# Pads that move the matmul operands of a two-layer encoder trunk to 0 or 32 modulo 256 bytes

## The chip, the core and the metric

The kernel runs on one core of a Trainium2 chip. The metric is the time of one execution in microseconds (us). TensorE multiplies: it first loads a stationary tile of 128x128 (a weight load, PEld in the profile) and then streams a moving tile past it (a matmul, PE). VectorE (DVE), ScalarE (ACT), GpSimd (POOL) and the queue of SyncE (SP), which issues the loads, work beside it. All operands lie in the on-chip memory, 128 partitions wide; an address here is a byte offset within a partition, the same in all of them.

## The reference

Two layers over 256 tokens of width 2048, all in float32. Layer 0 mixes tokens with a convolution module, layer 1 with latent attention; behind each comes an MLP with squared ReLU, and an RMS norm stands before each sub-layer and at the end.

```python
for layer in range(2):
    h = rms_norm(x, norm_mixer_g[layer])
    if layer == 0:   # h @ w_pw1, GLU, causal depthwise conv (width 31), layer norm, swish, @ w_pw2
        x = x + conv_module(h, ...)
    else:            # low-rank q and kv, rotary key, 16 heads, block-causal mask, @ w_o
        x = x + mla(h, cos, sin, ...)
    h = rms_norm(x, norm_mlp_g[layer])
    x = x + jnp.square(jax.nn.relu(h @ mlp_w1[layer])) @ mlp_w2[layer]   # 2048 -> 8192 -> 2048
return rms_norm(x, final_norm_g)
```

## The kernel before

**Products in three parts.** TensorE's one-pass format (float32r) keeps fewer bits than float32. So each operand is split in a high part and the rest (`hi` and `lo` of the weights, `xh`/`xl`, `gh`/`gl`, `sh`/`sl_`, `kvh`/`kvl`, `qh`/`ql`, `oh`/`ol` of the activations), and a product is high by high, low by high and high by low, summed in one accumulator. `mm3` (L177 to L179) does this with activations stationary and weights moving:

```python
nc.tensor.matmul(ps, sh, mh, start=start, stop=False)   # L177
nc.tensor.matmul(ps, sl, mh, start=False, stop=False)   # L178
nc.tensor.matmul(ps, sh, ml, start=False, stop=stop)    # L179
```

**Weights.** Each weight comes in units of up to 1 MB. SP loads a unit into one of three `raw` buffers. ScalarE copies it to `hi` (L151), VectorE (POOL in the first stage) subtracts to get `lo` (L152), in halves, with six buffers for each. The loads run ahead as buffers come free; the order of instructions on the engines is the order of the program.

**Stages.**
- First convolution product (L479 to L481, 1536 matmuls of 256 columns): weights stationary, `xh`/`xl` (tile `xt`) moving. Beside it run the depthwise taps in full float32 (L512 on TensorE, tiles `dg` and `ub`; the rest on VectorE).
- Second convolution product (384 matmuls of 512 columns): `sh`/`sl_` stationary, weights moving. Half of it runs in the convolution's own loop, half in `product_A`.
- MLP, twice. The first product is 1024 pairs a layer: a 512-wide matmul of `hi` against `xh` and `xl` side by side (L394), then a 256-wide one of `lo` against `xh` (L395). The squared ReLU gives `gh`/`gl`. The second product is `product_A`, 1536 `mm3` matmuls a layer, 512 wide, `gh`/`gl` stationary, weights moving.
- Attention: the input product on `xt` as stationary (192 matmuls of 288 columns and 96 of 512); the up-projections with `kvh`/`kvl` and `qh`/`ql` (moving in L964 to L966 and L987 to L989, stationary in `mm3`; 672 matmuls of 256 columns); scores and values in full float32 on the tiles of pool `gp`; and the output product with `oh`/`ol` stationary (384 matmuls of 512 columns), part of it between the heads, part in `product_A`.

In `product_A` the innermost loop is

```python
for j in range(4):
    k = 4 * u + j
    for t in range(T):
        mm3(ps[t], hi(k, t), lo(k, t), *wjs[u](j), k == 0, k == nk - 1)
```

**Addresses.** Pools lie one behind the other on the left side of the memory; the pools opened with `side="right"` (`edge`, then `xt` or `gp`) grow down from the top. Two small tiles on the left (`pad_const`, `pad_small`) and one on the right (`pad_right`) hold nothing that is read; their sizes set where the next tiles begin. Nearly all steps inside a tile are multiples of 256 bytes, so that a tile's start modulo 256 is that of each slice. An exception is the weights of the attention's input product, whose two column halves are 1152 bytes apart.

| tiles | start modulo 256 before |
|---|---|
| weights `hi`, `lo` (behind `pad_const`) | 0 |
| `sh`, `sl_`, `gh`, `gl` (behind `pad_small`) | 128 |
| `xt`, and `kT`, `qT`, `qpT`, `vv`, `pT` in `gp` (below `pad_right`) | 128 |
| `kvh`, `kvl`, `qh`, `ql`, `kpT` | 0 |
| `oh`, `ol` | 0 |

Of the kernel before, what the change touches and what calls it, by code (L numbers as in the profile page):

```python
# [10 lines left out]
F32 = mybir.dt.float32  # L11
# [7 lines left out]
P = 128  # L19
# [15 lines left out]
CHUNK = 64  # L35
HALVES = 2
PAD_CONST = 24
PAD_SMALL = 16
PAD_RIGHT = 24
WB = 6  # L40
LOOK = WB // 2 - 1
PE_TAPS = (3, 3, 3, 3)
# [28 lines left out]
def trunk_kernel(  # L71
# [26 lines left out]
    nc = tc.nc  # L98
# [13 lines left out]
            psum[kind] = psum_cx[0].enter_context(tc.tile_pool(name=kind + name, bufs=n, space=PSUM, reuse_waits="tile"))  # L112

    ctx.callback(lambda: psum_cx[0].close())


    const.tile([P, PAD_CONST], F32, name="pad_const")
    small.tile([P, PAD_SMALL], F32, tag="pad_small", name="pad_small", bufs=1)
    edge = ctx.enter_context(tc.tile_pool(name="edge", bufs=1, side="right"))
    pad_right = edge.tile([P, PAD_RIGHT], F32, name="pad_right")  # L120
    nc.gpsimd.memset(pad_right, 0.0)
# [699 lines left out]
    with ExitStack() as cx:  # L821
        at = cx.enter_context(tc.tile_pool(name="at", bufs=1, reuse_waits="tile"))
# [63 lines left out]
        def u_load(n):  # L886
            if n < len(units):
                srcs, shape = units[n]
                raw = raws[n] = wpool.tile(shape, F32, tag="raw", name=nm("raw"), bufs=3)
                for i, src in enumerate(srcs):  # L890
                    dst = raw if len(srcs) == 1 else raw[:, i : i + 1, :]
                    if len(src.shape) == 4:
                        dst = dst.rearrange("p j (h n) -> p j h n", h=src.shape[2])
                    nc.sync.dma_start(dst, src)
# [18 lines left out]
        def prefetch(n=9):  # L913
            while pending and n > 0:
# [3 lines left out]
                if h == 1:  # L918
                    u_load(u + 3)

        kvh = at.tile([P, KR // P, S], F32R, name="kvh")
        kvl = at.tile([P, KR // P, S], F32R, name="kvl")
        qh = at.tile([P, QR // P, S], F32R, name="qh")
        ql = at.tile([P, QR // P, S], F32R, name="ql")
        kpT = at.tile([P, S], F32, name="kpT")
        oh = at.tile([P, H, S], F32R, name="oh")
        ol = at.tile([P, H, S], F32R, name="ol")

# [325 lines left out]
```

## Time and profile before

| | |
|---|---|
| time, median of 3 runs | 2067.19 us (2066.62 to 2067.25) |
| profiled execution | 2066.48 us, of which the span from the first to the last instruction is 2064.7 |
| TensorE busy | 99% of the span, 11132 matmuls and as many weight loads |
| granted TensorE clock | 0.998 |

In the profile, PE is the matmul, PEld its weight load. A row of a group gives line, engine, operation, output and inputs, shapes and count; then busy time in us, the mean ns of one, and the idle time ahead with what ended it. Matmuls overlap, so the mean of one is longer than the distance from one to the next. The timeline gives start and duration in us.

### The profile page before, as it was taken

The numbers are of one execution on the slowest core, as the hardware profiler recorded it, in microseconds if no ns is written. First come the engines' busy times: TensorE is split into PE (matmuls) and PEld (weight loads), VectorE is DVE, ScalarE is ACT, GpSimd is POOL, SyncE is SP. The second block draws the span as 40 slices with busy tenths as digits, with TensorE's granted clock in tenths as the row PEclk, the third lists the DMA queues.
The fourth block names the chain that finished last, engine by engine and source line by source line (L and its number), as shares of the span: only waits on it lengthen the run. The fifth ranks groups of instructions, "written<-read, shape, count | busy, mean of one in ns | idle before, by whom it ended". The sixth has DMA issues, their size and how long they took to land.

```text
span 2064.7 us, 27877 instructions
## 1 busy us (share of the span) xinstructions
PE 2041.7 (99%) x11132; PEld 1753.7 (85%) x11132; DVE 1217.6 (59%) x1820; ACT 951.7 (46%) x1325; POOL 173.3 (8%) x99
## 2 busy tenths in 40 slices
PE   7999999999999999999999999999999999999998
PEld 7999888888888888888889887888888888888886
DVE  5999866665544465555446655665654445565454
ACT  5444565544433354444445544554443334454442
POOL 5887300000000000000000000000000000000000
PEclk9999999999999999999999999999999999999999
DMA  7555355565555665555555344566655555555552
GB/s 231 164 164 164 123 185 183 185 188 193 188 184 190 191 190 184 185 192 187 179 166 165 107 138 147 190 197 190 194 185 185 191 193 186 184 185 192 193 184 102
DMA packets 243267, 367.59 MB, mean 178 GB/s; under 512 B 15416, under 2 KB 89792, under 8 KB 242880
## 3 DMA queue, kind: packets, MB, share of 16 engines
q1 hardware_dynamic: 242400, 364.68, 55.0%
q8 instruction: 87, 1.43, 0.3%
q10 hardware_dynamic: 736, 1.12, 0.2%
q14 instruction: 44, 0.36, 0.0%
HBM read 363.68 MB, written 2.10 MB: 177 GB/s over the span
## 4 chain that ended last, share of the span: by engine, by line
PE 98%; DVE 1%; DMA 0%; ACT 0%; issue 0%; SPq 0%; DVEq 0%; ACTq 0%
PE acc L394 23%; PE acc L177 16%; PE acc L179 16%; PE acc L178 16%; PE acc L395 12%; PE acc L481 3%; PE acc L480 3%; PE acc L479 3%; PE sum L512 1%; PE acc L1042 1%; PE tr L234 1%; PE acc L1041 1%; PE acc L964 0%; PE acc L987 0%; PE acc L966 0%; PE acc L965 0%
## 5 line engine op out<-in xcount | busy, mean ns | idle before, releaser
L152 DVE TENSOR_TENSOR lo<-raw,hi 128x1024 fp32r<-128x1024 f32 (+1 forms) x628 | 755.4, 1206 | 710.3 <-ACT hi L151 695.8
L151 ACT ACTIVATE hi<-raw 128x1024 fp32r<-128x1024 f32 (+1 forms) x696 | 722.0, 1045 | 820.3 <-PE acc L178 475.0
L394 PE MATMUL acc<-xt,hi 128*128 128x512 f32 x2048 | 719.5, 394 | 0.0
L395 PE MATMUL acc<-xt,lo 128*128 128x256 f32 x2048 | 579.4, 283 | 0.0
L394 PEld LDWEIGHTS acc<-xt,hi 128*128 128x128 f32 x2048 | 384.6, 188 | 88.7
L177 PE MATMUL acc<-hi,gh 128*128 128x512 f32 x1024 | 404.3, 395 | 0.0
L179 PE MATMUL acc<-lo,gh 128*128 128x512 f32 x1024 | 404.1, 395 | 0.0
L178 PE MATMUL acc<-hi,gl 128*128 128x512 f32 x1024 | 404.0, 395 | 0.0
L395 PEld LDWEIGHTS acc<-xt,lo 128*128 128x128 f32 x2048 | 385.0, 188 | 0.1
L179 PEld LDWEIGHTS acc<-lo,gh 128*128 128x128 f32 x1024 | 192.9, 188 | 45.0
L177 PEld LDWEIGHTS acc<-hi,gh 128*128 128x128 f32 x1024 | 192.9, 188 | 44.9
L178 PEld LDWEIGHTS acc<-hi,gl 128*128 128x128 f32 x1024 | 192.9, 188 | 44.9
L546 DVE SCALAR_TENSOR_TENSOR sum<-ub,w_dw,sum 128x256 f32<-128x256 f32 x402 | 167.7, 485 | 4.9 <-ACT sum L515 2.9
L152 POOL TENSOR_TENSOR lo<-raw,hi 128x1024 fp32r<-128x1024 f32 x68 | 161.6, 2398 | 60.1 <-ACT hi L151 60.1
L479 PE MATMUL acc<-xt,hi 128*128 128x256 f32 x512 | 148.3, 290 | 0.0
L481 PE MATMUL acc<-xt,lo 128*128 128x256 f32 x512 | 144.3, 282 | 0.6 <-POOL lo L152 0.6
L480 PE MATMUL acc<-xt,hi 128*128 128x256 f32 x512 | 144.2, 282 | 0.0
L481 PEld LDWEIGHTS acc<-xt,lo 128*128 128x128 f32 x512 | 96.4, 188 | 0.8 <-POOL lo L152 0.8
L480 PEld LDWEIGHTS acc<-xt,hi 128*128 128x128 f32 x512 | 96.5, 188 | 0.6 <-DVE xt L190 0.2
L479 PEld LDWEIGHTS acc<-xt,hi 128*128 128x128 f32 x512 | 96.5, 188 | 0.4
L402 ACT ACTIVATE v<-acc 128x256 f32<-128x256 f32 x128 | 46.8, 383 | 26.1 <-PE acc L395 26.1
L177 PE MATMUL acc<-hi,sh 128*128 128x512 f32 x128 | 51.3, 400 | 0.0
(198 smaller groups left out, 1673.0 us busy)
## 6 DMA issues: line engine op xcount, KB each, us to landing
raw<-in_mlp_w SPq DMA_DIRECT2D x256, 1024.0 KB, 5.1
raw<-in_conv_w_pw SPq DMA_DIRECT2D x64, 512.0 KB, 4.9
raw<-in_conv_w_pw SPq DMA_DIRECT2D x16, 1024.0 KB, 5.0
raw<-in_mla_w_o SPq DMA_DIRECT2D x16, 1024.0 KB, 5.5
raw<-in_mla_w_kv_up SPq DMA_DIRECT2D x8, 1024.0 KB, 5.4
raw<-in_mla_w_in SPq DMA_DIRECT2D x8, 576.0 KB, 3.7
raw<-in_mla_w_in SPq DMA_DIRECT2D x4, 1024.0 KB, 4.9
raw<-in_mla_w_q_up SPq DMA_DIRECT2D x16, 256.0 KB, 3.2
```

The lines of the kernel that those rows point to most:

```text
L151: nc.scalar.activation(hi, raw[:, js, :], AF.Copy)
L152: eng.tensor_tensor(lo, raw[:, js, :], hi.bitcast(F32), op=ALU.subtract)
L177: nc.tensor.matmul(ps, sh, mh, start=start, stop=False)
L178: nc.tensor.matmul(ps, sl, mh, start=False, stop=False)
L179: nc.tensor.matmul(ps, sh, ml, start=False, stop=stop)
L394: nc.tensor.matmul(ps[b], wh[:, bs], xhl(k), start=k == 0, stop=False)
L395: nc.tensor.matmul(ps[b][:, :S], wl[:, bs], xh(k), start=False, stop=k == KC - 1)
L402: nc.scalar.activation(v[:, b, :], o[:, S:], AF.Copy)
L479: nc.tensor.matmul(o, wh[:, bs], xh(k), start=k == 0, stop=False)
L480: nc.tensor.matmul(o, wh[:, bs], xl(k), start=False, stop=False)
L481: nc.tensor.matmul(o, wl[:, bs], xh(k), start=False, stop=k == KC - 1)
L546: nc.vector.scalar_tensor_tensor(out=out, in0=ubs[c][:, w : w + S], scalar=tap(c, w), in1=pcs[c], op0=ALU.mult, op1=ALU.add)
```

## The change

Three constants get another size, and two pad tiles are put into the attention's pool, each cleared once by POOL. No other instruction changes.

```diff
-PAD_SMALL = 16
-PAD_RIGHT = 24
+PAD_SMALL = 48
+PAD_RIGHT = 48
+PAD_KV = 40
+PAD_O = 56
...
+        pad_kv = at.tile([P, PAD_KV], F32, name="pad_kv")
+        nc.gpsimd.memset(pad_kv, 0.0)
         kvh = at.tile([P, KR // P, S], F32R, name="kvh")
         kvl = at.tile([P, KR // P, S], F32R, name="kvl")
         qh = at.tile([P, QR // P, S], F32R, name="qh")
         ql = at.tile([P, QR // P, S], F32R, name="ql")
         kpT = at.tile([P, S], F32, name="kpT")
+        pad_o = at.tile([P, PAD_O], F32, name="pad_o")
+        nc.gpsimd.memset(pad_o, 0.0)
         oh = at.tile([P, H, S], F32R, name="oh")
         ol = at.tile([P, H, S], F32R, name="ol")
```

By the sizes (four bytes an element), `sh`, `sl_`, `gh` and `gl` move from 128 to 0, `xt` and the tiles of `gp` from 128 to 32, `kvh`, `kvl`, `qh`, `ql` and `kpT` from 0 to 32; `hi`, `lo`, `oh` and `ol` stay at 0. The stationary address minus the moving one, modulo 256:

| product | before | after |
|---|---|---|
| first convolution product, first MLP product (weights stationary, `xt` moving) | 128 | 224 |
| second convolution product, second MLP product (`mm3`) | 128 | 0 |
| attention's input product (`xt` stationary) | 128, for the second column half 0 | 32, second half 160 |
| up-projections, weights stationary | 0 | 224 |
| up-projections, weights moving | 0 | 32 |
| attention's output product | 0 | 0 |

## The prediction

> **What bounds the kernel now.** I read the page's busy shares and its chain first, then the groups of instructions with the shapes kept apart, then the timeline of TensorE alone, in which the starts of neighbouring matmuls give what the durations hide.
>
> ```profile
> span 2064.7 us, 27877 instructions
> PE 2041.7 (99%) x11132; PEld 1753.7 (85%) x11132; DVE 1217.6 (59%) x1820; ACT 951.7 (46%) x1325; POOL 173.3 (8%) x99
> POOL 5887300000000000000000000000000000000000
> GB/s 231 164 164 164 123 185 183 185 188 193 188 184 190 191 190 184 185 192 187 179 166 165 107 138 147 190 197 190 194 185 185 191 193 186 184 185 192 193 184 102
> PE 98%; DVE 1%; DMA 0%; ACT 0%; issue 0%; SPq 0%; DVEq 0%; ACTq 0%
> core 0: 2064.7 us, clock 0.998
> ```
>
> The chain that ended last is TensorE for 98%, at a granted clock of 0.998. No other engine has to be mended: the time is the sum of the distances from one matmul's start to the next (its pitch), and a change that moves only addresses can act on nothing else.
>
> ```profile
> L152 DVE TENSOR_TENSOR lo<-raw,hi 128x1024 fp32r<-128x1024 f32 x604 | 737.9, 1225 | 690.8 <-ACT hi L151 676.4 <-PE tr L234 10.1 <-DMA raw<-in_mla_w_kv_up 2.4
> L394 PE MATMUL acc<-xt,hi 128*128 128x512 f32 x2048 | 719.5, 394 | 0.0
> L151 ACT ACTIVATE hi<-raw 128x1024 fp32r<-128x1024 f32 x672 | 706.2, 1059 | 800.5 <-PE acc L178 455.3 <-PE acc L394 310.8 <-ACT gh L406 29.3
> L178 PE MATMUL acc<-hi,gl 128*128 128x512 f32 x1024 | 404.0, 395 | 0.0
> L178 PE MATMUL acc<-hi,ol 128*128 128x512 f32 x128 | 49.9, 390 | 0.0
> ```
>
> The last two rows are the same instruction on the same shape: one line, 512 columns, 128x128 stationary. One takes 395 ns, the other 390. In the first the stationary tile `gl` lies at 128 modulo 256 bytes, in the second `ol` lies at 0; the moving weights lie at 0 in both. I call D the stationary address minus the moving one, modulo 256: 128 in the first row, 0 in the second. Durations overlap, so I take pitches from the timeline (start in us, duration, operation). The second MLP product, 62 rows, 61 steps:
>
> ```profile
> 559.77 0.39 PE L178 MATMUL acc<-hi,gl 128*128 128x512 f32 x1
> ...
> 573.95 0.40 PE L179 MATMUL acc<-lo,gh 128*128 128x512 f32 x1
> ```
>
> 14.18 / 61 = 232.5 ns at D = 128. The attention's output product, 34 rows, 33 steps, D = 0:
>
> ```profile
> 1304.32 0.39 PE L178 MATMUL acc<-hi,ol 128*128 128x512 f32 x1
> ...
> 1311.80 0.39 PE L178 MATMUL acc<-hi,ol 128*128 128x512 f32 x1
> ```
>
> 7.48 / 33 = 226.7 ns. So the trace already holds both layouts in the same loop (`product_A`), and D = 0 is 5.8 ns a matmul cheaper. The Trainium skill, page "TensorE: Matmul & The Clock Gate", section "Part 2: What happens when you issue a matmul", says that the stationary and the moving operand have independent read ports, so that loading the next stationary tile takes nothing from the running matmul. By that rule alone D could not matter and the time would stay at 2067; these two pitches disagree with it by 5.8 ns.
>
> **The change part by part.** Pads alone move; no instruction on TensorE, ScalarE, VectorE or in a queue is added or dropped but two memsets on POOL. By the sizes of the pads: PAD_SMALL adds 128 bytes ahead of everything behind the small pool, PAD_RIGHT takes 96 bytes off everything on the right side, `pad_kv` (160) and `pad_o` (224) shift the attention's tiles.
>
> *1. Second MLP product, 3072 matmuls (L177 to L179 on gh, gl).* Stationary 128 becomes 0, moving stays 0: D goes from 128 to 0, the pair of addresses of the oh rows. 3072 x 5.8 = 17.8 us off the path. The other end: D = 0 isn't always at 226.7. Behind a break the pitch stays higher for a while (9 rows, 8 steps):
>
> ```profile
> 1270.99 0.40 PE L179 MATMUL acc<-lo,oh 128*128 128x512 f32 x1
> ...
> 1272.84 0.39 PE L178 MATMUL acc<-hi,ol 128*128 128x512 f32 x1
> ```
>
> 1.85 / 8 = 231.3 ns, a gain of 1.2 ns, 3.7 us in all if the matmuls never settled. I take 17.8: the loop of the 1304 us rows is the very loop that term 1 runs, and there it had settled.
>
> *2. Second convolution product, 384 matmuls (sh, sl).* The same move, D 128 to 0: 384 x 5.8 = 2.2 us (0.5 at 1.2 ns).
>
> *3. First MLP product, 2048 pairs of a 512- and a 256-wide matmul (L394, L395).* Here the weights are stationary at 0 and xt moves: 128 becomes 32, D goes from 128 to 224. No row has D = 224 in this shape. Now, 30 rows of L394, 29 pairs:
>
> ```profile
> 399.72 0.39 PE L394 MATMUL acc<-xt,hi 128*128 128x512 f32 x1
> 399.94 0.28 PE L395 MATMUL acc<-xt,lo 128*128 128x256 f32 x1
> 400.06 0.40 PE L394 MATMUL acc<-xt,hi 128*128 128x512 f32 x1
> 400.30 0.28 PE L395 MATMUL acc<-xt,lo 128*128 128x256 f32 x1
> ...
> 409.90 0.40 PE L394 MATMUL acc<-xt,hi 128*128 128x512 f32 x1
> ```
>
> 10.18 / 29 = 351.0 ns a pair; the 512-wide ones swing between 0.22 and 0.24 us in one and the same layout, so a good part of the price is where in time the weight load meets the stream, not the bytes alone. 256-wide at D = 0 (key and value up-projection, 51 rows, 50 steps) and at D = 128 (first convolution product, 45 rows, 44 steps):
>
> ```profile
> 1112.10 0.28 PE L964 MATMUL acc<-kvh,hi 128*128 128x256 f32 x1
> ...
> 1118.10 0.28 PE L966 MATMUL acc<-kvh,lo 128*128 128x256 f32 x1
> ```
> ```profile
> 99.72 0.28 PE L480 MATMUL acc<-xt,hi 128*128 128x256 f32 x1
> ...
> 104.94 0.28 PE L479 MATMUL acc<-xt,hi 128*128 128x256 f32 x1
> ```
>
> 6.00 / 50 = 120.0 ns and 5.22 / 44 = 118.6 ns. D = 224 is 32 bytes from D = 0 and 96 from D = 128, so I price it as D = 0, its nearest row: 226.7 + 120.0 = 346.7 ns a pair, 4.3 ns off, 2048 x 4.3 = 8.9 us. Ends: a stream that isn't disturbed at all. The nearest row is the taps' product in full fp32, which reads its moving columns twice, each matmul with its own weight load:
>
> ```profile
> 34.33 1.29 PE sum L512 x6
> ```
>
> 1.29 / 6 = 215 ns for what amounts to 512 columns, about 108 for 256: a pair of 323, 57 us off. The other end: every 512-wide one at the slow beat of the rows above (400.06 to 400.30, 0.24 us) beside 0.12: 360 a pair, 18 us more.
>
> *4. First convolution product, 1536 matmuls 256 wide (L479 to L481).* Also D 128 to 224, by the same row 120.0 for 118.6: 1.4 x 1536 = 2.2 us more. Ends: 108 (16 us off) and the same 1.4 ns once again (4.3 us more).
>
> *5. Low-rank up-projections of the attention, 672 matmuls 256 wide (kvh, kvl, qh, ql).* D goes from 0 to 224 where they move and to 32 where they are stationary; the pitch is 120.0 now and I leave it: 0. Ends: 8 us off at 108, 0.9 us more at 1.4 ns each.
>
> *6. Attention's input product.* 192 matmuls 288 wide; their moving half-rows are 1152 bytes apart, so that D alternates between 128 and 0 already (47 rows, 46 steps):
>
> ```profile
> 1073.53 0.29 PE L179 MATMUL acc<-lo,xt 128*128 128x288 f32 x1
> ...
> 1079.66 0.30 PE L177 MATMUL acc<-hi,xt 128*128 128x288 f32 x1
> ```
>
> 133.3 ns each, whichever D: 0. The 96 that are 512 wide go from D = 128 to 32: 0, within 0.6 us. Scores, values, taps and transposes shift with both operands or run at half speed: 0. The output product's oh and ol stay at 0: 0.
>
> *7. The memsets of the two pads.* POOL is idle from the eighth slice on (the POOL row), nothing is queued behind them there, and no matmul reads the pads: 0. Without that cover some 2.6 us, by POOL's nearest simple operation:
>
> ```profile
> L686 POOL TENSOR_TENSOR xs<-xs,b 128x512 f32<-128x512 f32 x8 | 10.4, 1295 | 0.0
> ```
>
> *What is late next.* A unit of weights (1 MB) feeds 24 matmuls of 226.7 = 5.4 us. ScalarE needs 2 x 1.06 and VectorE 2 x 1.23 us for it, and both stand idle 691 to 800 us in these lines. 1 MB in 5.4 us is 193 GB/s; the first slice moved 231. So the supply keeps up.
>
> Sum: -17.8 - 2.2 - 8.9 + 2.2 = -26.7 us. The profiled run took 2066.5 us (its span is 2064.7), 0.7 under the median of 2067.2: 2039.8 for it, 2040.5 for the median.
>
> **The rivals.**
>
> *A. The 32-byte offset does more than D = 0.* For it: taps show that a weight load and a stream can pass at 215. Against: no row of a one-pass matmul is there. Halfway to the floor: 512 wide at 221, 256 wide at 114, a pair of 335: -32.8, convolution -7.1, up-projections -4.0, with -20.0 of terms 1 and 2: 2067.2 - 63.9 = 2003.
>
> *B. D = 224 acts as D = 128 does*, and only the stationary moves pay (terms 1 and 2): 2067.2 - 20.0 = 2047. For it: at 256 columns D = 0 and 128 differ by only 1.4 ns, so the offset may matter in few places.
>
> *C. The address isn't the cause.* The oh rows might be quick because of what else runs there. Against: same loop, same loads and splits beside it. Then 2067. The rule quoted above would say the same.
>
> *D. Slower.* A stream that starts at 32 modulo 256 begins inside what may be a larger unit of reading. 6016 matmuls would have such a moving operand (4096 + 1536 + 384). It decides from 20.0 / 6016 = 3.3 ns each; at 5.8 ns, what 128 bytes do above, it is +34.9 - 20.0: 2082. For it: every one-pass stream of the trace starts at 0 or 128, so it's untried. Against: the taps' streams start at 4-byte steps and hold 215.
>
> **How the numbers follow.** Forecast 0.46, A 0.22, B 0.18, C 0.06, D 0.08. A measurement of this kernel can tell about 0.2%, 4 us. Faster are the forecast, A and B: 0.86; C is the same: 0.06; D slower: 0.08. The forecast's own range is 2033 to 2046 (its terms 3 to 5 within 6 us). The range for 8 in 10 takes in B and the nearer half of A and leaves out C, D and the far end of A: 1998 to 2053.
>
> **What would show it.** Right: L177 to L179 on gh and gl at 390 instead of 395 ns and a pitch near 226.7; L394 with L395 at 347 a pair; the first convolution product near 120. Rival A would show L394 well under 390 ns and a pair near 335, B the old 351, D more than 355. Term 1 is wrong if the gh pitch stays near 231, as behind the break at 1271 us. The chain should stay TensorE at 98%; a new idle time before L177 or L394 released by VectorE or DMA would mean that the supply had become late after all.

## The result, and the profile after

The changed kernel runs in 2034.74 us (median of four, 2034.44 to 2036.34) against 2067.07 (four runs, 2066.62 to 2067.25): 32.3 us less, a ratio of 0.9845 with a 95% interval of 0.9828 to 0.9863. The profiled execution took 2034.44 us, its span is 2032.6, 32.1 below the span of before. The page of after, its busy shares and its chain:

```profile
span 2032.6 us, 27882 instructions
PE 2009.5 (99%) x11132; PEld 1747.1 (86%) x11132; DVE 1214.8 (60%) x1820; ACT 951.7 (47%) x1325; POOL 174.2 (9%) x101
PE 98%; DVE 1%; DMA 0%; ACT 0%; issue 0%; SPq 0%; DVEq 0%; ACTq 0%
```

As many matmuls and weight loads as before, TensorE still 98% of the chain, VectorE and ScalarE within 3 us of what they were. The 32 us are TensorE's own. The groups of instructions, shapes kept apart (the three lines of `mm3` are L180 to L182 now, the first MLP product's L397 and L398):

```profile
L397 PE MATMUL acc<-xt,hi 128*128 128x512 f32 x2048 | 710.5, 390 | 0.0
L398 PE MATMUL acc<-xt,lo 128*128 128x256 f32 x2048 | 577.7, 282 | 0.0
L180 PE MATMUL acc<-hi,gh 128*128 128x512 f32 x1024 | 398.6, 389 | 0.0
L181 PE MATMUL acc<-hi,gl 128*128 128x512 f32 x1024 | 398.4, 389 | 0.0
L182 PE MATMUL acc<-lo,gh 128*128 128x512 f32 x1024 | 398.4, 389 | 0.0
```

The `gl` row has come from 395 to 389 ns, to within 1 ns of what the `ol` row of the same line had all along. L398 tells of the limit of such rows: 283 became 282, while its pitch fell by 2.2. So here too the pitch is read from the timeline of TensorE (start in us, duration, operation). The second MLP product, 63 rows, 62 steps:

```profile
544.80 0.39 PE L181 MATMUL acc<-hi,gl 128*128 128x512 f32 x1
...
558.86 0.39 PE L180 MATMUL acc<-hi,gh 128*128 128x512 f32 x1
```

14.06 / 62 = 226.8 ns, where it was 232.5. The first MLP product, 30 rows of L397, 29 pairs:

```profile
399.89 0.39 PE L397 MATMUL acc<-xt,hi 128*128 128x512 f32 x1
400.12 0.28 PE L398 MATMUL acc<-xt,lo 128*128 128x256 f32 x1
400.24 0.39 PE L397 MATMUL acc<-xt,hi 128*128 128x512 f32 x1
...
409.95 0.39 PE L397 MATMUL acc<-xt,hi 128*128 128x512 f32 x1
```

10.06 / 29 = 346.9 ns a pair instead of 351.0. The first convolution product, 51 rows, 50 steps:

```profile
99.12 0.28 PE L482 MATMUL acc<-xt,hi 128*128 128x256 f32 x1
...
104.96 0.28 PE L484 MATMUL acc<-xt,lo 128*128 128x256 f32 x1
```

5.84 / 50 = 116.8 ns instead of 118.6. And the up-projection with `kvh` moving, 24 rows, 23 steps:

```profile
1098.53 0.28 PE L971 MATMUL acc<-kvh,hi 128*128 128x256 f32 x1
...
1101.21 0.28 PE L973 MATMUL acc<-kvh,lo 128*128 128x256 f32 x1
```

2.68 / 23 = 116.5 ns instead of 120.0. Summed over the whole timeline, from the start of each matmul of a product to the start of the next matmul (us; in brackets the mean in ns):

| product | before | after | difference | predicted |
|---|---|---|---|---|
| second MLP (3071 steps) | 714.1 (232.5) | 696.5 (226.8) | -17.6 | -17.8 |
| second convolution (384) | 90.3 (235.2) | 88.3 (229.9) | -2.0 | -2.2 |
| first MLP, 512 wide (2048) | 472.4 (230.7) | 467.9 (228.5) | -4.5 | |
| first MLP, 256 wide (2048) | 247.0 (120.6) | 242.5 (118.4) | -4.5 | -8.9 for both |
| first convolution (1536) | 189.1 (123.1) | 186.6 (121.5) | -2.5 | +2.2 |
| up-projections (672) | 82.8 (123.2) | 81.4 (121.2) | -1.3 | 0 |
| attention's input product, output product, all else | 250.5 | 251.0 | +0.5 | 0 |

These means are over the whole product, breaks included, so they lie above the settled pitches where blocks are short. Nothing has become late in exchange: the longest wait of TensorE in the view of waits is still the load at the start, and the next is 1.2 us.

```profile
PE tr L276 <- DMA stage<-in_conv_b_dw: 8.6, 1, 8.6
PE sum L515 <- DVE ub L500: 1.2, 1, 1.2
```

### The profile page after: what moved, and what is told of

Its sections match the earlier page's. It is cut to its first block, busy times and chain, and to the rows that moved or that the text cites. A ratio compares the mean times of both kernels' runs of the same rounds, so it can differ in the third digit from the quotient of the medians.

```text
span 2032.6 us, 27882 instructions
## 1 busy us (share of the span) xinstructions
PE 2009.5 (99%) x11132; PEld 1747.1 (86%) x11132; DVE 1214.8 (60%) x1820; ACT 951.7 (47%) x1325; POOL 174.2 (9%) x101
## 4 chain that ended last, share of the span: by engine, by line
PE 98%; DVE 1%; DMA 0%; ACT 0%; issue 0%; SPq 0%; DVEq 0%; ACTq 0%
PE acc L397 23%; PE acc L180 16%; PE acc L182 16%; PE acc L181 16%; PE acc L398 12%; PE acc L482 3%; PE acc L484 3%; PE acc L483 3%; PE sum L515 1%; PE acc L1049 1%; PE tr L237 1%; PE acc L1048 1%; PE acc L971 0%; PE acc L994 0%; PE acc L972 0%; PE acc L973 0%
## 5 line engine op out<-in xcount | busy, mean ns | idle before, releaser
L397 PE MATMUL acc<-xt,hi 128*128 128x512 f32 x2048 | 710.5, 390 | 0.0
L398 PE MATMUL acc<-xt,lo 128*128 128x256 f32 x2048 | 577.7, 282 | 0.0
L397 PEld LDWEIGHTS acc<-xt,hi 128*128 128x128 f32 x2048 | 384.4, 188 | 80.5
L180 PE MATMUL acc<-hi,gh 128*128 128x512 f32 x1024 | 398.6, 389 | 0.0
L182 PE MATMUL acc<-lo,gh 128*128 128x512 f32 x1024 | 398.4, 389 | 0.0
L181 PE MATMUL acc<-hi,gl 128*128 128x512 f32 x1024 | 398.4, 389 | 0.0
L398 PEld LDWEIGHTS acc<-xt,lo 128*128 128x128 f32 x2048 | 387.1, 189 | 0.1
L182 PEld LDWEIGHTS acc<-lo,gh 128*128 128x128 f32 x1024 | 192.2, 188 | 40.1
L180 PEld LDWEIGHTS acc<-hi,gh 128*128 128x128 f32 x1024 | 192.2, 188 | 39.7
```

The source lines that it names most:

```text
L397: nc.tensor.matmul(ps[b], wh[:, bs], xhl(k), start=k == 0, stop=False)
L398: nc.tensor.matmul(ps[b][:, :S], wl[:, bs], xh(k), start=False, stop=k == KC - 1)
```

## The experiments

All but the one with half loads change nothing but pads and, in the last, where the pool of `xt` is opened again; each diff is against the changed kernel. Pitches are means over the whole product, worked out as in the table, unless a stretch of the timeline is shown. In brackets stands the time of before, measured beside it on the same chip.

**Which addresses count.** The theory was that D, the stationary address minus the moving one, is what matters, product by product; the rivals were that only one kind of move pays, or that the absolute start does.

Stationary moves alone (`gh`, `gl`, `sh`, `sl_` at 0; `xt` back at 128, `kvh` and its like at 0):

```diff
-PAD_RIGHT = 48
-PAD_KV = 40
-PAD_O = 56
+PAD_RIGHT = 24
+PAD_KV = 32
+PAD_O = 64
```

> PAD_SMALL alone takes effect: gh, gl, sh, sl at 0 (D = 0 in the second products); xt, kvh and qh stay where they were before. Theory 1 (the cost is set, product by product, by the difference D of the two operands' addresses): second MLP product at 226.8 ns a matmul (before 232.5), second convolution product 2 us shorter, first MLP product unchanged at 351.3 ns a pair, first convolution product unchanged at a mean of 123.1; time 2067.1 - 17.6 - 2.0 = 2047.5 us. Theory 2 (the parts are coupled: the layout as a whole sets how TensorE meets the other engines): the gain is not this part of 32.3 us, and the first products move too.

2047.30 us (2047.11 to 2049.06; before 2066.75), ratio 0.9908 (0.9893 to 0.9923). Its groups:

```profile
L397 PE MATMUL acc<-xt,hi 128*128 128x512 f32 x2048 | 719.6, 394 | 0.0
L180 PE MATMUL acc<-hi,gh 128*128 128x512 f32 x1024 | 398.8, 389 | 0.0
```

The second MLP product is at its pitch of after (226.8 ns), the first at that of before (351.3 a pair), in one kernel.

Moving addresses alone (`xt` at 32; `gh`, `gl`, `sh`, `sl_` back at 128, `kvh` at 0):

```diff
-PAD_SMALL = 48
-PAD_KV = 40
-PAD_O = 56
+PAD_SMALL = 16
+PAD_KV = 64
+PAD_O = 64
```

> PAD_RIGHT alone takes effect: xt at 32 (D = 224 in the first products); gh, gl, sh, sl stay at 128, kvh and qh at 0. Theory 1 (D, product by product): first MLP product at 346.9 ns a pair (before 351.3), first convolution product 2.5 us shorter, second MLP product unchanged at 232.5; time 2067.1 - 9.0 - 2.5 = 2055.6 us. Theory 2 (coupled layout): some other time, and the second products move too.

2055.41 us (2054.97 to 2056.84; before 2066.75), ratio 0.9947 (0.9931 to 0.9964):

```profile
L397 PE MATMUL acc<-xt,hi 128*128 128x512 f32 x2048 | 710.6, 390 | 0.0
L180 PE MATMUL acc<-hi,gh 128*128 128x512 f32 x1024 | 404.4, 395 | 0.0
```

The mirror image: 346.9 a pair, 232.5 in the second product. The two gains, 19.5 and 11.3, add up to 30.8 of the 32.3; the up-projections, at D = 0 in both of these, account for 1.3 more. So each product pays for its own layout.

Every address up by 32, every D as in the changed kernel:

```diff
-PAD_CONST = 24
-PAD_RIGHT = 48
+PAD_CONST = 32
+PAD_RIGHT = 40
```

> Every operand tile 32 bytes higher than in the changed kernel (weights at 32, gh and sh at 32, xt and kvh at 64): all differences D as in the changed kernel, no address as there. Theory 1 (D alone counts): every product keeps the changed kernel's pitch within 0.3 ns, time 2034.7 us within 2. Theory 3 (the residue of one operand counts, such as a stream that starts at 0): the second MLP product, whose stream now starts at 32 instead of 0, leaves 226.8 ns; at the pitch before, 232.5, it would be 17.5 us longer, 2052 us.

2034.98 us (2034.75 to 2035.30; before 2066.75), ratio 0.9847 (0.9832 to 0.9861):

```profile
L397 PE MATMUL acc<-xt,hi 128*128 128x512 f32 x2048 | 710.6, 390 | 0.0
L180 PE MATMUL acc<-hi,gh 128*128 128x512 f32 x1024 | 398.8, 389 | 0.0
```

Here the streams of both MLP products start at other addresses than in the changed kernel, 3072 of them at 32 rather than 0, and both pitches stay. So for this shift, the only one tried, what counts is the difference D and not where a stream begins.

**Whose D: a matmul's own, or that of the tile loaded beside it.** A tile of 160 bytes between the `hi` and the `lo` buffers of the weights gives the matmuls with `lo` another D than their neighbours (128 for 224 in the first MLP product, 96 for 0 in the second):

```diff
+        if "pad_lo" not in psum:
+            psum["pad_lo"] = wpool.tile([P, PAD_LO], F32, tag="pad_lo", name="pad_lo", bufs=1)
+            nc.gpsimd.memset(psum["pad_lo"], 0.0)
...
-PAD_SMALL = 48
+PAD_SMALL = 72
+PAD_LO = 40
```

> The changed kernel with a pad of 160 bytes between the high and the low weights: lo at 160, all else where it is in the changed kernel. In the first MLP product the 512-wide stream runs beside the load of lo and uses hi; the 256-wide stream runs beside the load of the next hi and uses lo. Theory 1a (what counts is the tile being loaded beside the stream): the 512-wide one has D = 128 now and goes from 228.5 to some 230.7 ns, the 256-wide one stays at 118.4. Theory 1b (what counts is the stationary tile that the stream itself uses): the 512-wide one stays at 228.5 and the 256-wide one goes from 118.4 to some 120.6. In the second MLP product only the matmul that streams lo (one of three) has another D, 96: its pitch alone should move, by an unknown amount, and the other two stay at 226.7.

2058.03 us (one run; before 2066.75):

```profile
L401 PE MATMUL acc<-xt,hi 128*128 128x512 f32 x2048 | 712.8, 392 | 0.0
L402 PE MATMUL acc<-xt,lo 128*128 128x256 f32 x2048 | 573.6, 280 | 0.0
L184 PE MATMUL acc<-hi,gh 128*128 128x512 f32 x1024 | 403.2, 394 | 0.0
L185 PE MATMUL acc<-hi,gl 128*128 128x512 f32 x1024 | 406.5, 397 | 0.0
L186 PE MATMUL acc<-lo,gh 128*128 128x512 f32 x1024 | 401.0, 392 | 0.0
```

Only L186 has another D in the second product, yet all three lines lost: by pitch L184 takes 231.5 ns, L185 234.5, L186 230.9, where each took 226.8. In the first product the 512-wide matmul lost 1.5 ns and the 256-wide one, whose D was changed, gained 0.4. That is nearer to what was expected if the tile loaded beside the stream counts (230.7 and 118.4) than if the tile in use does (228.5 and 120.6). But for the second product either theory had two of the three lines stay. The question has no clean answer because its premise fell: the pitch isn't a matmul's own. One odd D in three changed the pitch of the whole loop.

**How the pitch depends on D.** Six kernels, each with one D for the first products (MLP and convolution) and one for the second:

```diff
 # PAD_SMALL, PAD_RIGHT, PAD_KV: 48, 48, 40 in the changed kernel
+56, 56, 32   # first product D = 0,   second D = 32
+40, 64, 48   # first D = 32,  second D = 224
+64, 72, 24   # first D = 64,  second D = 64
+32, 40, 56   # first D = 192, second D = 192
+24, 32, 64   # first D = 160, second D = 160
+72, 80, 16   # first D = 96,  second D = 96
```

> The changed kernel with xt at 0 (first products: D = 0 instead of 224) and gh, sh at 32 (second products: D = 32 instead of 0). The step of the prediction that priced D = 224 as D = 0 is tested by the first. Theory 4 (the price grows with the distance of D from 0, either side): first MLP product 345 to 347 ns a pair (226.7 + 120.0, or less), second MLP product at 228.5, the pitch of D = 224 in the changed kernel: +5 us, time about 2040 us. Theory 5 (the price depends on the sign: a load that starts just behind the stream differs from one just ahead): D = 32 leaves the 228.5 clearly, to 231 or more: 2048 us or more; and the first convolution product, 117 ns at D = 224, goes to 120 at D = 0, 4 us more.

2070.67 us (one run; before 2068.70). This is the test of the prediction's step for term 3, since the first MLP product stands at D = 0 here:

```profile
L397 PE MATMUL acc<-xt,hi 128*128 128x512 f32 x2048 | 720.7, 398 | 0.0
L180 PE MATMUL acc<-hi,gh 128*128 128x512 f32 x1024 | 405.4, 396 | 0.0
```

The mean pair costs 351.9 ns, and it isn't one number. The timeline early in the first MLP product (33 rows of L397, 32 pairs), then further on in the same product (33 rows, 32 pairs):

```profile
399.78 0.40 PE L397 MATMUL acc<-xt,hi 128*128 128x512 f32 x1
...
410.87 0.40 PE L397 MATMUL acc<-xt,hi 128*128 128x512 f32 x1
```
```profile
759.67 0.40 PE L397 MATMUL acc<-xt,hi 128*128 128x512 f32 x1
...
770.98 0.40 PE L397 MATMUL acc<-xt,hi 128*128 128x512 f32 x1
```

11.09 / 32 = 346.6 and 11.31 / 32 = 353.4 ns: two beats of the same instructions at the same D. (A beat here is a sequence of pitches that a loop repeats.) The quicker one holds through the first half of layer 0's product; its second half and both halves of layer 1's are at the slower.

> The changed kernel with xt at 224 (first products: D = 32) and gh, sh at 224 (second products: D = 224). Theory 4 (distance of D from 0): D = 32 as D = 224 in the first MLP product, 346.9 ns a pair, and the second MLP product at 228.5: +5 us, 2040 us. Theory 5 (sign counts): the second MLP product still 227 to 228.5, the first at another pitch than 346.9, 350 or more: 2047 us or more.

2072.67 us (one run; before 2068.70), 4.0 above before:

```profile
L397 PE MATMUL acc<-xt,hi 128*128 128x512 f32 x2048 | 724.1, 397 | 0.0
L180 PE MATMUL acc<-hi,gh 128*128 128x512 f32 x1024 | 404.9, 395 | 0.0
```

D = 224 in the second product takes 233.4 ns, more than the 232.5 of before, though it is one of the two best in the first; D = 32 in the first takes 353.5 a pair. That the cost grows with the distance from D = 0, and that a D good for one product is good for the other, are both refuted by these pitches. The time itself comes from one run on each side.

> The changed kernel with xt at 192 and gh, sh at 64: D = 64 in the first and in the second products. Theory 4: between D = 0 and D = 128: second MLP product 229.6 ns, first MLP product 349 a pair: +8.6 +4.3 us, about 2048 us. Theory 5: anything, and other than D = 192 on the same product.

2067.31 us (one run; before 2068.70):

```profile
L397 PE MATMUL acc<-xt,hi 128*128 128x512 f32 x2048 | 724.1, 398 | 0.0
```

353.5 a pair, 233.4 in the second product; but the first convolution product, with the same operands as the first MLP product in another order, has its best mean here (119.6 ns).

> The changed kernel with xt at 64 and gh, sh at 192: D = 192 in the first and in the second products. Theory 4: the same as D = 64, about 2048 us. Theory 5: other than D = 64; if D = 224 is the low point of the first products, D = 192 lies between 346.9 and 351.3 ns a pair there.

2056.47 us (one run; before 2068.70):

```profile
L181 PE MATMUL acc<-hi,gl 128*128 128x512 f32 x1024 | 399.0, 390 | 0.0
L180 PE MATMUL acc<-hi,gh 128*128 128x512 f32 x1024 | 401.5, 392 | 0.0
```

The only other D at which the second product gains: 229.0 ns. The first is at 353.5 a pair.

> The changed kernel with xt at 96 and gh, sh at 160: D = 160 in the first and in the second products. By the points so far (second MLP product 226.8 at D = 0, 233.4 at 32 and 64, 232.5 at 128, 229.0 at 192, 233.4 at 224; first MLP product a pair 351.9 at 0, 353.5 at 32, 64 and 192, 351.3 at 128, 346.9 at 224) the distance of D from 0 says nothing. Theory 6 (most D leave the matmuls unsettled at one common price, and single values of D let them fall into a shorter beat): 232 to 234 and 351 to 354. Theory 4 (nearness): between the values at 128 and 192: 230.8 and 352.4.

2068.27 us (one run; before 2067.22): 350.3 a pair, 233.4 in the second product. The first is just below the 351 to 354 of the theory of one common price, and neither is at the value between its neighbours (352.4 and 230.8).

> The changed kernel with xt at 160 and gh, sh at 96: D = 96 in the first and in the second products. Theory 6 (single values of D let the matmuls fall into a shorter beat, the others cost one common price): second MLP product 232 to 234, first MLP product 351 to 354 a pair, time about 2066 us. Theory 4 (nearness): 233.0 and 352.4.

2061.12 us (one run; before 2067.22):

```profile
L397 PE MATMUL acc<-xt,hi 128*128 128x512 f32 x2048 | 710.6, 392 | 0.0
L180 PE MATMUL acc<-hi,gh 128*128 128x512 f32 x1024 | 406.2, 397 | 0.0
```

346.9 a pair, exactly as at D = 224, and the worst second product of all, 234.3 ns. The value at 96 also answers for the kernel with `lo` at 160: if each matmul paid for its own D, two at 0 and one at 96 would have a mean of (2 x 226.8 + 234.3) / 3 = 229.3 ns, and the mean there was 232.3. The 351 or more expected for the first product were wrong, as was every guess from a neighbour before. All eight D, mean pitch in ns (128 is the kernel before; 0 in the second product and 224 in the first products are the changed kernel; each number is from one trace):

| D | second MLP, one | first MLP, a pair | first convolution, one |
|---|---|---|---|
| 0 | 226.8 | 351.9 | 124.1 |
| 32 | 233.4 | 353.5 | 122.4 |
| 64 | 233.4 | 353.5 | 119.6 |
| 96 | 234.3 | 346.9 | 122.2 |
| 128 | 232.5 | 351.3 | 123.1 |
| 160 | 233.4 | 350.3 | 124.2 |
| 192 | 229.0 | 353.5 | 122.0 |
| 224 | 233.4 | 346.9 | 121.5 |

A D that is quick for one product can be slow for another. Read block by block (half a layer's first product is a block), the settled pair of the first MLP product has few values: 346.7 ns at 96, at 224 and in the quick block at 0; 353.3 or 353.4 at 32, 64, 192 and in the three slow blocks at 0; 350.0 at 160 and 351.1 at 128. At D = 0 the loop runs in the beat of either group. So D doesn't fix the pitch alone, and a D with a single trace might show another beat in another run. The 346.7 at 224 and the 226.7 of the second product at 0 came back in every trace with that layout.

**Is it the length of the weight load?** In `product_A`, all steps of k but the first and the last use half of the stationary columns, so that half of the output's rows are only partly summed:

```diff
+wd = lambda k: P if k in (0, nk - 1) else P // 2
-mm3(ps[t], hi(k, t), lo(k, t), *wjs[u](j), k == 0, k == nk - 1)
+mm3(ps[t][: wd(k), :], hi(k, t)[:, : wd(k)], lo(k, t)[:, : wd(k)], *wjs[u](j), k == 0, k == nk - 1)
```

> The changed kernel, in which the second products of the MLP (and the loop part of the others that share it) load only 64 of the 128 stationary columns for all but the first and the last row block: half of the output rows miss most of their sum. Streams, addresses and D are the changed kernel's. Theory L (the time above the undisturbed 215 ns is lost where the load of the next stationary tile and the stream meet): half a load meets half as often, 11.8 ns fall to about 6, second MLP product at 221 ns. Theory S (the stream itself or the step from one matmul to the next costs it): 226.8 stays.

2045.29 us (one run; before 2067.22). The timeline of the weight loads and of the matmuls (56 rows, 55 steps):

```profile
555.20 0.14 PEld L180 LDWEIGHTS acc<-hi,gh 128*64 128x64 f32 x1
...
557.96 0.19 PEld L180 LDWEIGHTS acc<-hi,gh 128*128 128x128 f32 x1
```
```profile
544.85 0.39 PE L182 MATMUL acc<-lo,gh 128*64 128x512 f32 x1
...
557.49 0.39 PE L180 MATMUL acc<-hi,gh 128*64 128x512 f32 x1
```

The load fell from 0.19 to 0.14 us, the pitch rose from 226.8 to 12.64 / 55 = 229.8 ns. Neither theory had it: a cost in proportion to the load would have lowered the pitch, a cost that ignores it would have left it. But the edit does two things: with 64 stationary columns the matmul also writes 64 output rows instead of 128 (`128*64` in its rows). Which of the two raised the pitch isn't told apart; what is shown is that a shorter load did not bring it down.

**The best D of each product.** The convolution's `xt` at D = 64, the MLP's at 224:

```diff
-PAD_RIGHT = 48
+PAD_RIGHT = 72
+PAD_XT = 40
...
+        if pad:   # in open_xt(name, pad=True), behind the tile xt in its pool
+            nc.gpsimd.memset(pool.tile([P, PAD_XT], F32, name=nm("pad_xt")), 0.0)
...
-    open_xt("xt0")
+    open_xt("xt0", False)
...
+        open_xt("xt0b")   # before the residual stage, so that the MLP's xt has the pad
```

> Each product at the best D measured so far: the changed kernel, in which xt lies at 192 during the first convolution product (D = 64) and at 32 from there on (D = 224 in the first MLP product, D = 0 in the second products, as in the changed kernel). Theory 1 (every product has its own price by its own D, and they add): first convolution product at a mean of 119.6 ns instead of 121.5, 1536 x 1.85 = 2.8 us less, all else as in the changed kernel: 2034.7 - 2.8 = 2031.9 us. Theory 2 (coupled layout, or the second opening of the xt pool makes the residual stage wait): 2034 us or more, or the first MLP product leaves 346.9 ns a pair.

2032.27 us (five runs, 2031.26 to 2032.95; before 2066.63), ratio 0.9832 (0.9819 to 0.9846). The first convolution product takes 184.4 us, 2.2 less than after; all other products are as after. The two intervals overlap, so the runs alone don't set it apart from the changed kernel; the profile's product does. It gained less than the 2.8 of the sweep. Its blocks fall in one of two beats, as the first MLP product's did at D = 0; so do those of the sweep's kernel at D = 64, but there about a third of the settled stretches are in the slower beat, here about half. Two stretches of its timeline, 57 rows (56 steps) and 49 rows (48 steps):

```profile
98.94 0.28 PE L485 MATMUL acc<-xt,hi 128*128 128x256 f32 x1
...
105.53 0.28 PE L487 MATMUL acc<-xt,lo 128*128 128x256 f32 x1
...
112.03 0.28 PE L485 MATMUL acc<-xt,hi 128*128 128x256 f32 x1
...
117.47 0.28 PE L485 MATMUL acc<-xt,hi 128*128 128x256 f32 x1
```

6.59 / 56 = 117.7 and 5.44 / 48 = 113.3 ns.

## Why the prediction was right, and where it was not

**Terms 1 and 2 (second products): right in mechanism and size.** -17.6 and -2.0 us. The trace of before held both layouts in the same loop, and the pitch read there was the pitch that came. The lower end, the 231.3 of the rows behind a break, didn't come about: the mean over all 3071 steps is 226.8, so what is lost behind breaks weighs next to nothing.

**Term 3 (first MLP product): the time came out, the step behind it was wrong.** The forecast priced D = 224 "as D = 0, its nearest row", 346.7 ns a pair; 346.9 was measured. But that pair is 228.5 + 118.4, not 226.7 + 120.0, and at D = 0 itself three quarters of the pairs cost 353.4. D = 192 and D = 32, the other neighbours of 224 and of 0, cost 353.5. Had the change set D to 0 here, the same step would have forecast 8.9 us of gain and the mean would have given 351.9 a pair, a loss of some 1.2 us on 2048 (351.3 before). The agreement to 0.1 us is a coincidence of the sum.

**Terms 4 and 5: the same step, and here it shows.** Priced by the 120.0 of D = 0, the first convolution product was to lose 2.2 us and gained 2.5; the up-projections were to stay and gained 1.3. Together these are 4.7 + 1.3 = 6.0 us beyond the forecast sum of 26.7; the span fell by 32.1, that is 5.4 beyond it, and the small remainders of the table's other rows give back the difference. Both lie within the ends of their terms.

**Terms 6 and 7** held: the attention's input product moved by 0.2 us, and the memset of a pad took 132 ns on POOL, which had stood idle.

```profile
L925 POOL MEMSET pad_kv<- 128x40 f32 x1 | 0.1, 132 | 772.6 <-PE acc L182 772.6
```

**What is late next** held as well: with a unit consumed every 5.4 us, no load and no split became a wait.

**The rivals.** A (halfway to an undisturbed stream) is out: in no layout was the second MLP product's mean pitch below 226.8 or the first's mean pair below 346.9. Only matmuls 256 wide come near A's 114 ns, in one of the two beats at D = 64 (113.3). A's floor, 215 and 108 ns, rests on counting 256 columns in full float32 as 512 in one pass; no run shows that it can be reached in one pass. B (only the stationary moves pay) is out by the kernel with the moving addresses alone: the first products gain there, and it is 11.3 us faster. D (a stream from 32 costs more) is out by the kernel with every address up by 32, where 3072 streams start at 32 and hold 226.8. C (the address isn't the cause) is out by the whole sweep, in which nothing but addresses changes and the time runs from 2034 to 2073.

On C, the Trainium skill's rule of independent read ports (page "TensorE: Matmul & The Clock Gate", section "Part 2: What happens when you issue a matmul") doesn't agree with these runs. By that rule alone the difference between the two addresses has no effect; the measured pitch of one 512-wide matmul goes from 226.8 to 234.3 ns with it.

**Open.** Why D matters. It is shown that moving D and nothing else moves the pitch, that a shift of all addresses by 32 bytes doesn't, and that the effect differs by product. D is not the whole of it, since two beats were seen at one D, and that 256 is the right modulus was assumed throughout and not tested. That the weight load and the stream meet in the memory at certain phases would fit, as the prediction read the 0.22 and 0.24 us of the pairs, but no run shows it, and whether the tile of the same matmul or the one loaded for the next is concerned isn't told apart.

## What to carry to other kernels

Where TensorE is the bound, read the pitch, from start to start, and not the duration, and look in the trace for the same shape in two layouts: that pair priced 20 us of this change to within 0.4. A few hundred bytes of padding are worth trying for each product separately, since a product's gain stands by itself and the wrong pad gains nothing (four of the six pads of the sweep, one run each, were within 0.2% of before). In a single product the wrong pad costs: 234.3 ns against the 232.5 of before. Don't carry a price from one D to the next, nor from one loop to another: what is measured is the rhythm of a whole sequence of matmuls.

## What was not expected of the hardware

- **Beats.** A loop locks in a rhythm that repeats within 1 ns: in the first MLP product the 512-wide pitches are 229, 228, 228 after and 234, 233 or 234, 224 before, over and over.
- **Two beats at one layout.** 346.6 and 353.4 ns a pair at D = 0 in one execution, 113.3 and 117.7 ns in the convolution at D = 64. Which one a block falls into wasn't controlled here.
- **Half the stationary columns made the loop slower**: weight loads of 0.14 us in place of 0.19, half the output rows, and 229.8 ns of pitch in place of 226.8.
- **One odd D among three** cost all three: 230.9 to 234.5 ns rather than 226.8, in one run.
